# Softmax factors of three head pairs: from a fan copy and four transposes to one transpose, a store to DRAM and two reads

## The chip, the cores and the metric

The kernel runs on one core of one Trainium2 chip. The metric is the device time of one execution in microseconds (us). The core's engines are TensorE (PE; its weight loads are PEld), VectorE (DVE), ScalarE (ACT), GpSimd (POOL) and SyncE (SP). SyncE, GpSimd and ScalarE also issue DMAs; SyncE's and ScalarE's go through hardware queues (q1 and q10 in the profile), GpSimd's through the software queue (q0). All of them are served by the same 16 DMA engines.

## The reference

One layer of a hybrid encoder over 512 positions of width 1024, in float32:

```
h = rms_norm(x, attn_norm_g)
xr, gate, q, k, v = split(h @ w_in)
y_rnn  = (rg_lru forward + rg_lru backward of conv(xr)) * gelu(gate)
y_attn = dilated_attention(q, k, v, rel_bias)        # 8 heads of 64, three windows each
x = x + concat(rms_norm(y_rnn), rms_norm(y_attn)) @ w_out
x = x + square(relu(rms_norm(x) @ w_up)) @ w_down
return rms_norm(x, final_norm_g)
...
# inside dilated_attention, for each window (offs, bias):
logits = q . k[gathered] * scale + bias;  lse = logsumexp(logits)
out_w = softmax(logits) . v[gathered]
# the windows are joined with the weights softmax(lse)
o = sum_w softmax(lse)_w * out_w
```

Joined with those weights, the three windows are one softmax over all gathered keys. The kernel computes it so: exponentials of all keys, their product with v, and at the end one division by the row's sum. The factor of that division, one number for each position and head, is what this case is about.

## The kernel before, in words

Matrix products are made in three passes of split operands (`whi`, `wlo` and the like, lines 329 to 331). ScalarE makes the high part of each weight tile (L274), VectorE the low part (L282), and SyncE streams the raw tiles in (L241), a fixed number ahead. The order of instructions on PE, ACT, DVE and POOL is the order in which the code is written (`manual_schedule`); SyncE's order is set by a scheduler, and is fixed in the built program.

The attention part handles heads in pairs, p = 0 to 3. A loop over i (0 to 4) and u (0 to 3) interleaves three stages: the scores and exponentials of pair i (`att_s`, `att_f`, `att_e`), the transposes of pair i-1 (`att_t`) and the product of pair i-1 with the values (`att_av`, at the end of step u = 3). Between them `fill` puts single steps of other matrix products (`pqk`, `pwr`) on TensorE. `pt`, `prow` and, for pairs 0 and 1, `pav` share two PSUM banks; `pav` and `prow` of the later pairs share two others.

The factors of a pair p take this way. The exponentials leave their sums in `zs[p]`, 128 rows (positions) by 8 columns (4 blocks of positions by 2 heads).

- `att_z(p)`, at step (p+1, 0): VectorE takes the reciprocal `rz` (128x8) and fans each column out 64 times into `rzb` (128x512, L854).
- `att_r(p)`, at step (p+1, 1): TensorE transposes `rzb` in four blocks of 128x128 into the bank `prow` (L408), and ScalarE copies it to `zrow[p]` (128x512, L861). Row r of `zrow` now holds, along its 512 positions, the factor of the head that row r of the value product belongs to.
- `att_av(p)`, at step (p+1, 3): 32 matmuls make the value product `pav`; then VectorE multiplies it with `zrow[p]` into `yp` (L952, in `av_y`). For pair 2 this multiplication is put off to step (4, 0), behind the next pair's first transposes (`late_y`). ScalarE squares and scales `yp` (L598, L957).

For pair 3 VectorE's order is: product of pair 2 (L952), reciprocal of pair 3 (L852), fan copy of pair 3 (L854); TensorE's transposes of pair 3 (L408) wait for that copy.

Other transfers in the same stretch: `load_x` (L1081 to L1089) loads residual tiles and builds three sums of weight blocks in the tile `ws`, with loads on SyncE and accumulating DMAs on GpSimd; `sum_s4` (L1094, L1095) copies one of them inside `ws` on SyncE and accumulates on GpSimd; `load_tw` (L479, L480) loads the bias rows `tb`; `load_t` (L1198, L1200) loads weights of the next stage.

Of the kernel before, what the change touches and what calls it, by code (L numbers as in the profile page):

```python
# [12 lines left out]
FT = mybir.dt.float32  # L13
FR = mybir.dt.float32r
AF = mybir.ActivationFunctionType
OP = mybir.AluOpType

P = 128
S = 512
# [3 lines left out]
DH = 64  # L23
# [86 lines left out]
def hybrid_kernel(ctx: ExitStack, tc, xw, xn, w_in, w_v, w_out, w_up, w_dn, gates, vecs, rel, onehot, fg, out):  # L110
    nc = tc.nc
# [4 lines left out]
    dram = ctx.enter_context(tc.tile_pool(name="dram", bufs=1, space=bass.MemoryType.DRAM))  # L116
# [3 lines left out]
    act = nc.scalar.activation  # L120
# [3 lines left out]
    def g_(name, dt=FT, shape=(P, S)):  # L124
        return work.tile(list(shape), dt, name=name, tag="g", bufs=NG)

    def small(name, w):
        return work.tile([P, w], FT, name=name, tag="sm%d" % w, bufs=8)

    def ps_(name, tag):  # L130
        return psum.tile([P, S], FT, name=name, tag=tag, bufs={"pj": 4, "gs": 2, "et": 2}[tag])
# [15 lines left out]
    ident = consts.tile([P, P], FT, name="ident")  # L147
# [253 lines left out]
    def fan(t, c, n, w):  # L401
        base = t[:, c:c + 1]
        return bass.AP(tensor=base.tensor, offset=base.offset, ap=[base.ap[0]] + ([[1, n]] if n > 1 else []) + [[0, w]])

    def rows_of(cols, tag):
        pr = ps_("prow", tag)
        for tt in range(4):
            nc.tensor.transpose(pr[:, tt * P:(tt + 1) * P], cols(tt), ident)  # L408
        return pr
# [74 lines left out]
    halves = (slice(0, 64), slice(64, 128))  # L484
# [284 lines left out]
    et, en, zs = {}, {}, {}  # L769
# [78 lines left out]
    zrow, rzbs = {}, {}  # L848

    def att_z(p):  # L850
        rz = small("rz", 8)
        nc.vector.reciprocal(rz, zs.pop(p))  # L852
        rzb = g_("rzb")
        nc.vector.tensor_copy(rzb, fan(rz, 0, 8, DH))  # L854
        rzbs[p] = rzb

    def att_r(p):
        rzb = rzbs.pop(p)
        pr = rows_of(lambda tt: rzb[:, tt * P:(tt + 1) * P], "et" if p < 3 else "gs")
        zrow[p] = g_("zrow")  # L860
        act(zrow[p], pr, AF.Copy)  # L861

    def att_y(p):
# [289 lines left out]
    for i in range(5):  # L1153
        for u in range(4):
# [20 lines left out]
            if u == 0 and i >= 1:  # L1175
                att_z(i - 1)
# [4 lines left out]
            if u == 1 and i >= 1:  # L1181
                att_r(i - 1)
# [85 lines left out]
    for w in OSEQ:  # L1268
        for i in range(4):
            tt, k = i // 2, i % 2  # L1270
# [253 lines left out]
    for half in range(2):  # L1524
# [169 lines left out]
        for j in range(7 * NQ):  # L1694
            _, w, q = seq[j]
# [31 lines left out]
        if half == 1:  # L1727
# [27 lines left out]
            pr = ps_("pd", "pj")  # L1755
# [60 lines left out]
```

## Time and profile before

| | before |
|---|---|
| median of 3 runs (lowest, highest) | 531.61 us (530.47, 531.9) |
| the profiled execution's own time | 532.29 us |
| its span, first to last instruction | 530.5 us |
| mean granted TensorE clock | 0.997 |
| DMA in the span | 35740 packets, 108.30 MB, mean 204 GB/s |
| queues, share of 16 engines' span | q1 41.1%, q0 32.1%, q10 1.3% |

The attention part lies between about 100 and 185 us of the span. In a row of a timeline the columns are start (us), duration (us), engine, line and operation, output<-input, count, and in brackets the idle time before it with what ended it; a row ending in a larger count merges instructions, and its duration runs from the first to the last. The `q` behind an engine's name (SPq) means its DMA queue: the row is the issue of a DMA, not its transfer. A row of waits reads: who waited, for whom, us in total, times, longest. A row of windows gives for a stretch the busy us of PE, PEld, DVE, ACT and POOL with their counts, then the granted clock, the share of the DMA engines and GB/s. A row of the chain gives start, duration and what was running. In the chain a matmul's time ends with its result, so its rows stand up to 0.2 us behind those of the timeline.

### The profile page before, as it was taken

Reading aid. Unit: us, or ns where it says so; the run is one execution under the profiler, and the core shown is the slowest. Engines: PE = TensorE matmul, PEld = TensorE weight load, DVE = VectorE, ACT = ScalarE, POOL = GpSimd, SP = SyncE. Lnnn points to the kernel's source line nnn. Section 1 sums busy time; section 2 is a strip of 40 time slices with the busy share of each in tenths; the row PEclk is TensorE's granted clock in tenths of the full one; section 3 lists DMA queues with packets and bytes.
Section 4 is the critical chain, followed back from the end, with each engine's and each line's share of the span. In section 5 each row is a group of like instructions: output and inputs, shape, how many; then the busy total and the mean of one; then the engine's idle time right before and its main releaser. Section 6 shows DMA issues by size and latency. Waiting matters only on the chain.

```text
span 530.5 us, 9181 instructions
## 1 busy us (share of the span) xinstructions
PE 521.1 (98%) x3495; PEld 446.4 (84%) x3495; DVE 431.0 (81%) x710; ACT 361.1 (68%) x569; POOL 66.8 (13%) x96
## 2 busy tenths in 40 slices
PE   8999999999999999999999999999999999999995
PEld 7855888877777878899999888888999999888884
DVE  5799589588779898898779986879756987987885
ACT  7566968578678867586477755575567677655654
POOL 3340000000202121001210222001101200131000
PEclk9999999999999999999999999999999999999998
DMA  8798165585567989948395999986968496799704
GB/s 309 256 236 217 41 152 159 164 150 179 105 220 153 331 196 256 371 146 229 100 214 144 228 272 274 311 289 140 291 209 228 107 223 207 163 299 263 174 1 159
DMA packets 35740, 108.30 MB, mean 204 GB/s; under 512 B 4109, under 2 KB 7082, under 8 KB 35696
## 3 DMA queue, kind: packets, MB, share of 16 engines
q1 hardware_dynamic: 26000, 74.66, 41.1%
q0 software_dynamic: 8784, 31.76, 32.1%
q10 hardware_dynamic: 912, 1.30, 1.3%
q8 instruction: 27, 0.44, 0.3%
q14 instruction: 17, 0.14, 0.1%
HBM read 98.24 MB, written 4.21 MB: 193 GB/s over the span
## 4 chain that ended last, share of the span: by engine, by line
PE 92%; ACT 2%; DMA 2%; DVE 2%; SPq 1%; issue 0%; DVEq 0%; ACTq 0%
PE pu L331 10%; PE pu L330 10%; PE pu L329 10%; PE pd L330 10%; PE pd L331 10%; PE pd L329 9%; PE pqk L329 3%; PE pqk L331 3%; PE pqk L330 3%; PE pt L841 2%; PE pav L928 2%; PE pv L329 1%; PE pn L787 1%; PE pp L331 1%; PE pp L329 1%; PE pp L330 1%
## 5 line engine op out<-in xcount | busy, mean ns | idle before, releaser
L282 DVE TENSOR_TENSOR wlo<-wraw,whi 128x1024 fp32r<-128x1024 f32 x72 | 87.8, 1221 | 26.4 <-ACT whi L274 26.2
L274 ACT ACTIVATE whi<-wraw 128x1024 fp32r<-128x1024 f32 x69 | 72.9, 1058 | 41.1 <-PE pd L331 20.5
L330 PE MATMUL pd<-wlo,ah 128*128 128x512 f32 (+1 forms) x195 | 75.4, 386 | 0.0
L329 PE MATMUL pd<-whi,ah 128*128 128x512 f32 (+1 forms) x195 | 75.3, 386 | 0.0
L331 PE MATMUL pd<-whi,al 128*128 128x512 f32 (+1 forms) x195 | 75.3, 386 | 0.0
L274 ACT ACTIVATE whi<-tw 128x1024 fp32r<-128x1024 f32 x40 | 42.3, 1059 | 38.0 <-DMA tw<-in_w_up_dram 11.1
L331 PE MATMUL pu<-hh,wlo 128*128 128x256 f32 x224 | 63.5, 284 | 0.0
L330 PE MATMUL pu<-hl,whi 128*128 128x256 f32 x224 | 63.5, 284 | 0.0
L329 PE MATMUL pu<-hh,whi 128*128 128x256 f32 x224 | 63.5, 283 | 0.0
L282 DVE TENSOR_TENSOR wlo<-tw,whi 128x1024 fp32r<-128x1024 f32 x40 | 48.9, 1223 | 17.9 <-ACT whi L274 17.9
L329 PE MATMUL pu<-h2h,whi 128*128 128x256 f32 (+1 forms) x200 | 60.2, 301 | 0.0
L331 PE MATMUL pu<-h2h,wlo 128*128 128x256 f32 (+1 forms) x200 | 60.1, 301 | 0.0
L330 PE MATMUL pu<-h2l,whi 128*128 128x256 f32 (+1 forms) x200 | 60.1, 301 | 0.0
L329 PEld LDWEIGHTS pu<-hh,whi 128*128 128x128 f32 x224 | 43.1, 192 | 0.0
L330 PEld LDWEIGHTS pu<-hl,whi 128*128 128x128 f32 x224 | 43.1, 192 | 0.0
L331 PEld LDWEIGHTS pu<-hh,wlo 128*128 128x128 f32 x224 | 43.1, 192 | 0.0
L329 PEld LDWEIGHTS pd<-whi,ah 128*128 128x128 f32 x195 | 36.7, 188 | 7.4
L330 PEld LDWEIGHTS pd<-wlo,ah 128*128 128x128 f32 x195 | 36.6, 188 | 7.3
L331 PEld LDWEIGHTS pd<-whi,al 128*128 128x128 f32 x195 | 36.7, 188 | 7.3
L274 ACT ACTIVATE whi<-ts 128x1024 fp32r<-128x1024 f32 x24 | 25.5, 1061 | 24.7 <-PE pd L331 18.5
L330 PEld LDWEIGHTS pu<-h2l,whi 128*128 128x128 f32 x200 | 38.3, 192 | 1.3
L331 PEld LDWEIGHTS pu<-h2h,wlo 128*128 128x128 f32 x200 | 38.3, 192 | 1.3
(286 smaller groups left out, 1232.8 us busy)
## 6 DMA issues: line engine op xcount, KB each, us to landing
wraw<-in_w_up_dram SPq DMA_DIRECT2D x25, 512.0 KB
ts<-in_w_dn_dram POOLq DMA_DIRECT2D x24, 512.0 KB, 13.5
wraw<-in_w_dn_dram SPq DMA_DIRECT2D x24, 512.0 KB
tw<-in_w_up_dram SPq DMA_DIRECT2D x15, 512.0 KB
tw<-in_w_up_dram POOLq DMA_DIRECT2D x15, 512.0 KB, 8.3
wraw<-in_w_in_dram SPq DMA_DIRECT2D x13, 512.0 KB
ts<-in_w_dn_dram SPq DMA_DIRECT2D x8, 512.0 KB
tw<-in_w_dn_dram SPq DMA_DIRECT2D x8, 512.0 KB
```

The source lines that it names most:

```text
L274: act(hi, raws[i], AF.Copy)
L282: nc.vector.tensor_tensor(lo, r, f(splits[i][0]), op=OP.subtract)
L329: nc.tensor.matmul(o, lhsT=a[0], rhs=b[0], start=bool(first), stop=False, skip_group_check=on)
L330: nc.tensor.matmul(o, lhsT=a[0], rhs=b[1], start=False, stop=False, skip_group_check=on)
L331: nc.tensor.matmul(o, lhsT=a[1], rhs=b[0], start=False, stop=bool(last), skip_group_check=on)
L787: nc.tensor.matmul(pnear[p][e][r, o:o + k1 - k0], lhsT=q, rhs=raw[p, 1][halves[e], k0:k1], start=u == u0, stop=True, skip_group_check=True)
L841: nc.tensor.transpose(pt[:, i * P:(i + 1) * P], en[h][u][:, c * P:(c + 1) * P], ident)
L928: nc.tensor.matmul(o(half[e]), lhsT=v[:, h * DH:(h + 1) * DH], rhs=c(et[h, x]), start=first, stop=last, skip_group_check=True)
```

## The change

For pairs 0, 1 and 2 the fan copy goes. `rz` (128x8) is transposed once into 8 rows of 128; ScalarE copies these 8x128 numbers to `zt`; a DMA stores them in a small DRAM tile `zd` (4 KB); and two DMAs, one for each head, read them back into `zrow[p]`, each with 64 rows that all read the same 4 blocks of 128 numbers (the first step of the source is 0). The DMAs are issued by GpSimd for pairs 0 and 1 and by SyncE for pair 2. Pair 3 stays as it was.

```diff
     def att_z(p):
         rz = small("rz", 8)
         nc.vector.reciprocal(rz, zs.pop(p))
+        if p < 3:
+            rzbs[p] = rz
+            return
         rzb = g_("rzb")
         nc.vector.tensor_copy(rzb, fan(rz, 0, 8, DH))
         rzbs[p] = rzb
 
+    zd = [dram.tile([8, P], FT, name="zd%d" % i) for i in range(3)]
+
     def att_r(p):
         rzb = rzbs.pop(p)
-        pr = rows_of(lambda tt: rzb[:, tt * P:(tt + 1) * P], "et" if p < 3 else "gs")
         zrow[p] = g_("zrow")
+        if p < 3:
+            pr = ps_("prow", "et")
+            nc.tensor.transpose(pr[:8, :P], rzb, ident)
+            zt = g_("zt", shape=(8, S))
+            act(zt[:, :P], pr[:8, :P], AF.Copy)
+            q = nc.gpsimd if p < 2 else nc.sync
+            q.dma_start(zd[p], zt[:, :P])
+            for e in range(2):
+                q.dma_start(zrow[p][halves[e]].rearrange("p (u q) -> p u q", u=4),
+                            bass.AP(tensor=zd[p].tensor, offset=zd[p].offset + e * P, ap=[[0, DH], [2 * P, 4], [1, P]]))
+            return
+        pr = rows_of(lambda tt: rzb[:, tt * P:(tt + 1) * P], "gs")
         act(zrow[p], pr, AF.Copy)
```

On SyncE's queue, before, the copy inside `ws` is followed at once by loads of weights (`wraw`, `tw`):

```order
L1094 DMA ws_1769<-ws_1769 128x1024
L241 DMA wraw_1981<-in_w_out_dram 128x1024
L1198 DMA tw_2351<-in_w_up_dram 128x1024
L241 DMA wraw_2051<-in_w_out_dram 128x1024
L1198 DMA tw_2376<-in_w_up_dram 128x1024
```

And now, with the store and the two reads of pair 2 (L871, L873; lines behind the edit are 16 higher):

```order
L1110 DMA ws_1770<-ws_1770 128x1024
L871 DMA zd2_873<-zt_1970 8x128
L873 DMA zrow_1967<-zd2_873 64x4x128 x2
L241 DMA wraw_1981<-in_w_out_dram 128x1024
L1214 DMA tw_2351<-in_w_up_dram 128x1024
L241 DMA wraw_2051<-in_w_out_dram 128x1024
```

The three DMAs of pair 2 stand behind the copy inside `ws` and ahead of the weight loads; the reads wait for the store's landing, and the weight loads stand behind both.

On GpSimd's queue, before, from the sums for the recurrent half (`tw`) to the sums in `ws`:

```order
L1050 DMA tw<-in_w_out_dram 128x1024 x3
L289 DMA tw<-in_w_out_dram 128x1024
L1050 DMA tw<-in_w_out_dram 128x1024
L416 TENSOR_TENSOR rcol_1610<-rv,mhalf 128x4
L1089 DMA ws<-in_w_out_dram 128x1024 x4
```

And now:

```order
L1066 DMA tw<-in_w_out_dram 128x1024 x3
L871 DMA zd_871<-zt 8x128
L873 DMA zrow<-zd_871 64x4x128 x2
L289 DMA tw<-in_w_out_dram 128x1024
L1066 DMA tw<-in_w_out_dram 128x1024
L416 TENSOR_TENSOR rcol_1610<-rv,mhalf 128x4
L871 DMA zd_872<-zt 8x128
L873 DMA zrow<-zd_872 64x4x128 x2
L1105 DMA ws<-in_w_out_dram 128x1024 x4
```

Pair 0's three DMAs stand ahead of the accumulate of L289, pair 1's ahead of the four accumulates into `ws`.

On VectorE, around the product of pair 2 (`yp_2099`; `rz_2101` and `rzb_2103` are of pair 3, which keeps its fan copy), as it stands now:

```order
L1054 SCALAR_TENSOR_TENSOR x1_1765<-pwr_2054,nrc0_1612,x1_1765 128x512
L968 TENSOR_TENSOR yp_2099<-pav_2068,zrow_1967 128x4x4x32
L852 RECIPROCAL rz_2101<-zz_1885 128x8
L857 COPY rzb_2103<-rz_2101 128x512
L282 TENSOR_TENSOR wlo_2130<-wraw_1368,whi_2062 128x1024
```

This row of instructions is the same as before; only the operand `zrow` of the product now comes from a DMA.

## The prediction

> **What bounds the kernel now.** I read the page's busy times first, then its chain, then the waits of SyncE's DMA queue, then the timeline around the four products that use the softmax factors.
>
> ```profile
> PE 521.1 (98%) x3495; PEld 446.4 (84%) x3495; DVE 431.0 (81%) x710; ACT 361.1 (68%) x569; POOL 66.8 (13%) x96
> ...
> PE 92%; ACT 2%; DMA 2%; DVE 2%; SPq 1%; issue 0%; DVEq 0%; ACTq 0%
> ```
>
> TensorE is busy for 98% of the span and is 92% of the chain that ended last. So only two things move the end: instructions taken off TensorE, and new waits of TensorE. Work taken off VectorE or ScalarE pays only where TensorE waits for it. The span is 530.5 us, the profiled execution's own time 532.29 us, the median of the three runs 531.61 us. I make the sum against 532.29 and take 0.68 off at the end.
>
> **What the change takes off TensorE.** The chain, in order of time, prices the transposes:
>
> ```profile
> 173.43 0.87 PE pt L841 x8
> ...
> 174.99 0.44 PE prow L408 x4
> ```
>
> Four transposes add 0.44 us to TensorE's stream, eight add 0.87 us, so one is 0.11 us. Each of the pairs 0, 1 and 2 loses three of four: 0.33 us a pair, about 1.0 us in all. The remaining one streams the same 128 columns of the identity and is priced the same.
>
> **What it takes off VectorE and ScalarE.** These rows, of a timeline of all engines, hold the fan copy (L854) and what surrounds the product of pair 2:
>
> ```profile
> 172.03 1.10 DVE L952 TENSOR_TENSOR yp<-pav,zrow 128x512 f32<-128x512 f32 x1
> ...
> 172.96 0.18 DVE L852 RECIPROCAL rz<-zz 128x8 f32<-128x8 f32 x1
> 173.19 0.43 DVE L854 COPY rzb<-rz 128x512 f32<-128x512 f32 x1
> ...
> 174.39 0.86 POOL L1095 DMA_DIRECT2D ws<-in_w_out_dram  x1 [9.64 <-DMA ws<-ws]
> ...
> 174.83 0.60 PE L408 MATMUL prow<-ident,rzb 128*128 128x128 f32 x4
> ```
>
> Three copies of 0.43 us go, and three ScalarE copies of 128x512 (about 0.6 us each) become copies of 8x128. TensorE is not waiting for either there, so I price both at nothing. Their cover is TensorE's own row of matmuls.
>
> **What it adds.** The factors reached the product's operand zrow by one ScalarE copy. Now they take three DMAs in sequence: a store of 4 KB, and two reads of 128 KB (256 pieces of 512 B each), which can be issued only after the store has landed. When the copy ran, and when pairs 0 and 1 needed it:
>
> ```profile
> 123.44 0.65 ACT L861 ACTIVATE zrow<-prow 128x512 f32<-128x512 f32 x1
> ...
> 143.74 0.65 ACT L861 ACTIVATE zrow<-prow 128x512 f32<-128x512 f32 x1
> ...
> 163.50 0.57 ACT L861 ACTIVATE zrow<-prow 128x512 f32<-128x512 f32 x1
> ```
>
> ```profile
> 133.65 1.11 DVE L952 TENSOR_TENSOR yp<-pav,zrow 128x512 f32<-128x512 f32 x1 [0.67 <-PE pav L928]
> ...
> 154.46 1.10 DVE L952 TENSOR_TENSOR yp<-pav,zrow 128x512 f32<-128x512 f32 x1 [0.67 <-PE pav L928]
> ```
>
> **Pairs 0 and 1, on GpSimd's queue.** From the start of the small copy to the product there are 10.2 us for pair 0 and 10.7 us for pair 1; the value products come 0.3 us earlier by the transposes saved, so 9.9 and 10.4 us. The nearest rows for a small transfer issued by GpSimd:
>
> ```profile
> oht<-in_onehot_dram POOLq DMA_DIRECT2D x1, 145.5 KB, 3.7
> oht<-in_onehot_dram POOLq DMA_DIRECT2D x1, 97.0 KB, 3.5
> ```
>
> The copy ends 0.3 us after it starts, the store takes 3.5, the second read is issued some 0.6 us after the first and takes 3.7: about 8.1 us. That leaves 1.8 us for pair 0 and 2.3 us for pair 1, so I price them at 0. What lies behind them on GpSimd's queue has room: the accumulate at L289 was issued at 132.85 and those at L1089 from 152.72. Bounds: nothing below. Above, a read of 9.0 us (a row below) ends pair 0 about 3.5 us late; VectorE then holds the bank of pav from the next transposes, and TensorE stands.
>
> **Pair 2, on SyncE's queue.** The order above shows its store behind the copy ws<-ws, which SyncE held back by 15.6 us until an accumulate had landed:
>
> ```profile
> SPq L1094 <- DMA ws<-in_w_out_dram: 15.6, 1, 15.6
> ```
>
> ```profile
> 167.62 0.53 SPq L1094 DMA_DIRECT2D ws<-ws  x1
> 168.25 0.72 SPq L241 DMA_DIRECT2D wraw<-in_w_out_dram  x1
> ```
>
> So although the factors of pair 2 are ready at about 163.8, their store starts at 167.6 at the earliest (167.62 + 0.53, less 0.6 for the transposes saved by then). The product ran at 172.03 without a wait in front of it. Four microseconds must hold a store and two reads.
>
> How long the store takes, no row says. The quick end is a store of 12 KB on an idle queue, whose reader waited for it:
>
> ```profile
> 64.30 0.91 ACTq L471 DMA_DIRECT2D nbd<-nbs  x2
> ```
>
> ```profile
> 65.76 1.30 SPq L479 DMA_DIRECT2D tb<-nbd  x2
> ```
>
> That is 1.5 us. The slow end is the transfer that this store directly follows in the same queue: ws<-ws was issued at 167.62, and GpSimd, which waited for its landing alone, went on at 174.39, so 6.8 us. The DMA engines are full there:
>
> ```profile
> 168.00:170.00 2.00, 2.00 (x22) 1.50 (x23) 2.00 (x7) 2.00 (x6) 0.00 (x0) 1.00 1.03 203
> ```
>
> With a share of 1.03 and a transfer of 512 KB ahead, I take the slow end: the store lands with ws<-ws, at 167.0 + 6.8 = 173.8. [...]
>
> For the reads the quick end is the 3.5 us above. The slow end is a bias read on SyncE's queue (tb, 128 KB in pieces of 1 KB) in another full stretch:
>
> ```profile
> 109.63 0.52 SPq L479 DMA_DIRECT2D tb<-nbd  x1
> ...
> 114.09 10.46 SPq L241 DMA_DIRECT2D wraw<-in_w_out_dram  x2
> ```
>
> ```profile
> SPq L241 <- DVE wlo L282: 5.5, 1, 5.5
> SPq L241 <- DMA tb<-nbd: 4.2, 1, 4.2
> ```
>
> The second of the two wraw issues waited 4.2 us for that tb from about 114.4, to 118.6: 9.0 us after its issue. I take 3.5, since everything else on SyncE's queue is now held back behind the reads. The second read is issued 0.5 us after the first, so zrow is whole at 173.8 + 0.5 + 3.5 = 177.8.
>
> Then the product, the reciprocal and the fan copy of pair 3 follow on VectorE, 1.6 us from 172.03 to 173.62, and the transposes of pair 3 (174.83 on TensorE) wait for that copy. They start at 179.4 + 0.06, which is **4.6 us later** than before. The 1.0 us saved on TensorE is inside this difference. Queued behind the product on VectorE are a weight split (wlo) and a residual update, whose readers come after those transposes; queued on ScalarE are the square and scaling of that product. On SyncE the weight loads that started from 168.25 start from about 175; the first is converted at 178.57, which moves to 183, and the rest later. I add nothing for them.
>
> Sum: 532.29 + 4.6 = 536.9, less 0.68 gives **536.2 us**. With the ends (169.1 or 173.8 for the store, 3.5 or 9.0 for the read), the shift lies between -0.1 and +10.1 us.
>
> **The rivals.**
>
> *The round trip is quick enough.* If the store passes ws<-ws and lands 1.5 us after its issue, the reads are whole at 173.1, pair 3's copy ends at 174.7, and TensorE, which is there at 173.85, stands 0.9 us, nearly what it has saved: 531.5. It decides at a landing of zrow near 173.2. For it: only 4 KB. Against it: 6.8 us for the transfer ahead and a full DMA share. [...]
>
> *No wait at all.* Only the transposes count: 531.61 - 1.0 = 530.6, within what a measurement here can tell from no change (0.3%, 1.6 us).
>
> *The clock falls in the stall.* TensorE would stand for about 5 us. At the end of the kernel the granted clock fell some 3.2 us after the last matmul (at 524.03; 0.63 over a microsecond is a fall at 527.26):
>
> ```profile
> 524.00:525.00 1.00, 0.03 (x1) 0.00 (x0) 0.96 (x5) 0.32 (x2) 0.00 (x0) 1.00 0.39 148
> ...
> 527.00:528.00 1.00, 0.00 (x0) 0.00 (x0) 0.00 (x0) 0.00 (x0) 0.00 (x0) 0.63 0.98 357
> 528.00:529.00 1.00, 0.00 (x0) 0.00 (x0) 0.00 (x0) 0.00 (x0) 0.00 (x0) 0.50 0.54 167
> ```
>
> If matmuls then run at half clock for as long as it took to fall, 3.2 us, half of that is lost: 1.6 us more, 537.8. No row shows how long the clock takes to recover, or whether a stall inside the kernel starts it. [...]
>
> *Pair 0 is late too.* Its reads run at 127 to 132, beside four residual loads and four bias reads of SyncE. If the second takes 6.5 us, pair 0 is about 1 us late and all of it lands on TensorE: 537.2.
>
> **How the numbers follow.** Stall at pair 2 alone: 0.50 (533.5 to 540). With the clock falling: 0.17, about a quarter of the stall's cases, since the one fall in the trace came after 3.2 us and the stall is little longer. With pair 0 late as well: 0.10. Quick round trip: 0.17. No wait: 0.06. The two last lie inside 530.0 to 533.2 but for a small tail, and the first three above it: faster 0.04, same 0.19, slower 0.77. The range takes in the quick round trip partly and the stall to 9 us: 531.2 to 540.8.
>
> **What the profile after would show.** Right: the product of pair 2 waits for a DMA of zrow for 4 to 7 us; the transposes of pair 3 wait for the fan copy; the store of pair 2 is issued within a microsecond after ws<-ws, and the reads 5 us or more later; products 0 and 1 wait for TensorE as before. Wrong: the reads of pair 2 issued by 170, or no wait before that product, or a wait at products 0 or 1 that is larger than that at product 2.

## The result and the profile after

| | before | after |
|---|---|---|
| median (lowest, highest) | 531.43 us (530.47, 531.9; 6 runs) | 544.62 us (541.87, 548.01; 6 runs) |
| ratio, with its 95% interval | | 1.0251 (1.0226 to 1.0275) |
| profiled execution's own time, span | 532.29 us, 530.5 us | 541.87 us, 540.1 us |
| mean granted clock of that execution | 0.997 | 0.991 |

The change costs 13.2 us in the medians, where the prediction had 4.6. The profiled execution of after is its lowest, that of before (532.29 us) lies above all six timed runs of its kernel, so the two profiles differ by 9.6 us only.

The busy times of the page after, and the shares of its chain:

```profile
PE 521.5 (97%) x3486; PEld 446.7 (83%) x3486; DVE 429.8 (80%) x707; ACT 360.9 (67%) x569; POOL 72.3 (13%) x102
...
PE 91%; DMA 4%; ACT 1%; DVE 1%; issue 0%; SPq 0%; DVEq 0%; ACTq 0%
```

TensorE is as busy as before in microseconds although nine transposes are gone (3495 and 3486 records), because some of its matmuls now run at half clock: the granted clock is 0.50 from 179.1 to 185.9 us, and the four transposes of pair 3 take about 418 ns each there, where before they take 272. DMA has doubled its share of the chain. The waits of VectorE and TensorE that are new:

```profile
DVE yp L968 <- DMA zrow<-zd: 13.6, 2, 10.1
...
PE prow L408 <- DVE rzb L857: 8.8, 1, 8.8
PE pt L841 <- DVE yp L968: 1.7, 1, 1.7
```

VectorE waits twice for the reads. TensorE's 1.7 us stand behind the product of pair 0 (the bank of `pav` comes free late), its 8.8 us behind that of pair 2 (pair 3's fan copy follows that product). The chain shows both places, in order of time:

```profile
128.08 6.13 DMA zrow<-zd
134.29 1.09 DVE yp L968
135.43 0.66 PE pt L841 x4
...
167.44 5.89 DMA zd<-zt
173.48 0.66 SPq L873
174.19 6.62 DMA zrow<-zd
180.93 1.08 DVE yp L968
182.08 0.44 DVE rzb L857
182.56 1.11 PE prow L408 x4
```

At pair 2 the store lands 5.9 us after its issue, the second read 6.6 us after its own. At pair 0 the reads are issued 5.3 us after the store, by these rows of GpSimd's timeline:

```profile
122.12 0.56 POOL L871 DMA_DIRECT2D zd<-zt  x1 [81.62 <-DMA tb<-nbd]
127.41 1.30 POOL L873 DMA_DIRECT2D zrow<-zd  x2 [4.73 <-DVE rsum L1001]
```

The second row names VectorE's `rsum` as what ended the wait. By the times it was the store: in the change the issue follows the store's last packet (126.3) by 1.1 us, and in eight kernels with this order, the change's included, it lies anywhere from 0.2 us before the end of `rsum` to 0.6 us behind it.

Four transposes behind a wait take 0.66 us at pair 0 and 1.11 us at pair 3. The windows say why (the column behind the five engines is the granted clock, then the DMA share and GB/s):

```profile
173.00:174.00 1.00, 0.79 (x4) 0.32 (x3) 0.00 (x0) 0.79 (x2) 0.33 (x1) 1.00 0.00 0
...
178.00:179.00 1.00, 0.00 (x0) 0.00 (x0) 0.00 (x0) 0.00 (x0) 0.00 (x0) 1.00 1.03 205
179.00:180.00 1.00, 0.00 (x0) 0.00 (x0) 0.00 (x0) 0.00 (x0) 0.00 (x0) 0.54 1.14 270
...
185.00:186.00 1.00, 1.00 (x5) 0.86 (x4) 0.52 (x2) 0.68 (x3) 0.00 (x0) 0.55 1.03 422
186.00:187.00 1.00, 1.00 (x7) 0.56 (x5) 0.59 (x2) 1.00 (x4) 0.00 (x0) 1.00 1.05 414
```

TensorE's last matmul ends at about 173.8. The clock falls to 0.50 at about 179.1, 5.3 us later, and comes back at about 185.9, 3.3 us after the matmuls resume at 182.56.

Two theories stood after this reading. A: the loss is two waits, a long one on SyncE's queue at pair 2 and a short one at pair 0, plus the clock that falls in the long one. B: a trip through DRAM costs wherever it is taken. In A it was open whether pair 2's lateness comes from its place in the queue or from reads that are slow in themselves, and what makes them slow.

### The profile page after: what moved, and what is told of

It reads as the page before. It is cut to its first block, busy times and chain, and to the rows that moved or that the text cites. A ratio compares the mean times of both kernels' runs of the same rounds, so it can differ in the third digit from the quotient of the medians.

```text
span 540.1 us, 9186 instructions
## 1 busy us (share of the span) xinstructions
PE 521.5 (97%) x3486; PEld 446.7 (83%) x3486; DVE 429.8 (80%) x707; ACT 360.9 (67%) x569; POOL 72.3 (13%) x102
## 4 chain that ended last, share of the span: by engine, by line
PE 91%; DMA 4%; ACT 1%; DVE 1%; issue 0%; SPq 0%; DVEq 0%; ACTq 0%
PE pu L329 10%; PE pu L331 10%; PE pu L330 10%; PE pd L329 9%; PE pd L330 9%; PE pd L331 9%; PE pqk L329 2%; PE pqk L331 2%; DMA zrow<-zd 2%; PE pqk L330 2%; PE pt L841 2%; PE pg L519 2%; PE pv L329 2%; PE pv L330 1%; PE pv L331 1%; PE pp L331 1%
## 5 line engine op out<-in xcount | busy, mean ns | idle before, releaser
L329 PEld LDWEIGHTS pu<-h2h,whi 128*128 128x128 f32 x200 | 38.3, 191 | 1.3
```

The lines of the kernel that those rows point to most:

```text
L329: nc.tensor.matmul(o, lhsT=a[0], rhs=b[0], start=bool(first), stop=False, skip_group_check=on)
```

## The experiments

Every ratio below is against the kernel before, timed beside it on the same chip.

### Which pair carries the loss

One part alone, three times. The condition in `att_z` and `att_r` is changed:

```diff
-        if p < 3:
+        if p < 2:      # pairs 0 and 1; in the two others  p == 2  and  p == 1
```

> Pairs 0 and 1 take the way through DRAM on GpSimd's queue, pair 2 keeps its fan copy and four transposes. Theory A (SyncE's queue at pair 2 carries nearly all of the loss, pair 0 carries one short stall of 1.7 us): six transposes less, -0.7 us, and the product of pair 0 about 1.7 us late, so about 532.4 us, between 531.3 and 533.5; no wait of VectorE or TensorE longer than 1 us between 165 and 190 us of the span. Theory B (the added traffic of the reads, or the way through DRAM as such, costs the same for every pair): a third to two thirds of the loss of 13 us is here, 536 to 540 us.

> Only pair 2 takes the way through DRAM, on SyncE's queue; pairs 0 and 1 are as before. Theory A: three transposes less (-0.3 us), TensorE stands about 8.8 us ahead of pair 3's transposes, the clock falls in that stall and costs about 1.7 us: +10 us, 541.5 us, between 539 and 545. Theory B (each pair carries its share): 536 us or less.

> Only pair 1 takes the way through DRAM, on GpSimd's queue, in a stretch where the DMA engines have little to do. All theories that put the loss on pairs 0 and 2: three transposes less, nothing waits, 0.3 us below the kernel before, which the runs cannot tell from no change. If the way through DRAM costs wherever it is taken: 533 us or more.

| | median | ratio |
|---|---|---|
| pairs 0 and 1 | 534.01 us | 1.0054 (1.0034 to 1.0074) |
| pair 2 | 544.35 us | 1.0251 (1.0230 to 1.0271) |
| pair 1 | 531.20 us | 0.9991 (0.9981 to 1.0001) |

Pair 2 alone has the whole ratio of the change, and pair 1 alone costs nothing. Pairs 0 and 1 lose 3.1 us, half a microsecond above the upper end that theory A gave. The two losses (13.4 and 3.1 us) do not add up to the change's 13.2. Part of that shows in the profiles: TensorE stands 9.3 us ahead of pair 3's transposes with pair 2 alone, 8.8 us in the change, where pair 0 has made it late already. The rest is not shown. The waits of that profile, which is its lowest run (532.64 us):

```profile
DVE yp L968 <- DMA zrow<-zd: 3.8, 1, 3.8
...
PE pt L841 <- DVE yp L968: 1.9, 1, 1.9
```

One wait for `zrow`, at pair 0, and 1.9 us of TensorE behind it. Theory B falls with pair 1: the same DMAs on the same queue, in a stretch where the DMA engines have little to do (in the change a share of 0.29 from 144 to 150 us, against 0.80 from 122 to 127 and 0.70 from 127 to 134 at pair 0), and no loss.

### The place on SyncE's queue

The copy `ws<-ws`, behind which pair 2's store stands, is issued by GpSimd instead:

```diff
-        nc.sync.dma_start(s4, s2)
+        nc.gpsimd.dma_start(s4, s2)
```

> The changed kernel with the copy inside ws issued by GpSimd, so that pair 2's store and reads stand on SyncE's queue behind nothing that waits. Theory A (the place in the queue, behind ws<-ws, is the cause): the store is issued at about 163 us, zrow is whole by 172 to 174, the product of pair 2 waits 0 to 2 us, the clock does not fall; with pair 0's 1.7 us and the 1.0 us saved the time is 532 to 534 us. Theory C (store and reads are slow in this stretch wherever they stand, 6 us each): zrow whole at about 176, TensorE stands 3 us or more, 535 to 538 us.

Measured: 536.40 us, ratio 1.0097 (1.0080 to 1.0114). In the timeline:

```profile
163.59 0.31 SPq L871 DMA_DIRECT2D zd<-zt  x1
165.58 1.36 SPq L873 DMA_DIRECT2D zrow<-zd  x2
...
177.14 1.08 DVE L968 TENSOR_TENSOR yp<-pav,zrow 128x512 f32<-128x512 f32 x1 [5.22 <-DMA zrow<-zd]
```

With nothing ahead of it the store lands within 2.0 us. But the reads, issued 8 us sooner than in the change, are whole only at 177.1, 10.2 us after the second was issued (165.58 + 1.36), and VectorE still waits 5.2 us for them. The place in the queue is half of the story. Theory C has the other half, the slow reads, but not the store, which it put at 6 us. What the DMA engines did from 166 to 174 us (queue, kind, packets, MB, share of 16 engines; q0 is GpSimd's, q1 SyncE's):

```profile
q0 software_dynamic: 387, 1.44, 94.0%
q1 hardware_dynamic: 245, 0.12, 7.9%
```

GpSimd's transfers, the accumulates into `ws` and from 169 the copy, take 94% of the engines' time, in packets of 3.7 KB on average that hold an engine 0.31 us each (0.94 x 16 x 8 / 387). SyncE's packets of 0.5 KB need 0.04 us each, and 245 of the reads' 512 pieces get through in 8 us.

### What makes the reads slow

Two runs. The first takes the competitor away: the changed kernel without the two DMAs of GpSimd that start with pair 2's reads.

```diff
-        nc.gpsimd.dma_start(s4, oblock("21"), accum_op=OP.add)
...
-        nc.gpsimd.dma_start(lo, raws[i], accum_op=OP.add)   # for the weight block s2 only
```

> The changed kernel without two of GpSimd's DMAs, the accumulate of a weight block into ws behind ws<-ws and the accumulating copy tw<-ws (512 KB each), so the weights built from them lack a term. In the changed kernel these run from 175 us, beside the reads of pair 2. Theory F (the reads are slow because the DMA engines are held by those accumulates): the reads land about 3.5 us after the last issue, as pair 1's did in a quiet stretch (3.2), not 6.6; TensorE stands about 6 us instead of 8.8, and the time is 2.5 to 4.5 us lower, 540 to 542 us. Theory E (a read of one small DRAM tile by 64 rows is slow of itself on SyncE's queue, or slowed by SyncE's own weight loads behind it): 6 us or more for the reads, and the time as with the change, 543.5 us or more.

Measured: 539.98 us, ratio 1.0152 (1.0133 to 1.0170), against 1.0251 for the change.

```profile
175.53 1.32 SPq L875 DMA_DIRECT2D zrow<-zd  x2
...
179.65 1.08 DVE L970 TENSOR_TENSOR yp<-pav,zrow 128x512 f32<-128x512 f32 x1 [6.76 <-DMA zrow<-zd]
```

The second read is issued by 176.85 and the product runs at 179.65, 2.8 us later instead of 6.1 by the same rows of the change (174.79 and 180.93). TensorE stands 5.5 us there instead of 8.8. Theory F holds: the accumulates made the reads slow. SyncE's own weight loads are issued behind the reads here too, and the reads took 2.8 us all the same.

The second makes the reads into fewer pieces. The reciprocal is written with the two heads apart, so that the 4 KB in DRAM lie by head and each of the 64 rows reads one piece of 2 KB:

```diff
-        nc.vector.reciprocal(rz, zs.pop(p))
+        nc.vector.reciprocal(rz.rearrange("p (e t) -> p t e", e=2), zs.pop(p).rearrange("p (t e) -> p t e", e=2))
...
-            bass.AP(tensor=zd[p].tensor, offset=zd[p].offset + e * P, ap=[[0, DH], [2 * P, 4], [1, P]]))
+            bass.AP(tensor=zd[p].tensor, offset=zd[p].offset + e * 4 * P, ap=[[0, DH], [1, 4 * P]]))
```

> The changed kernel with the factors stored in another order, so that each of the 64 rows of a read takes one piece of 2 KB instead of four of 512 B: the same bytes in a quarter of the pieces. Theory D (on each DMA engine the pieces of SyncE's queue take turns with the pieces of GpSimd's accumulates, which take 0.31 us each, so a read is as slow as it has pieces): the reads of pair 2 land 2 to 3 us sooner than the 6.6 us after the last issue, pair 0's 1.7 us go too, the store's 5.9 us stay; TensorE still stands 5 to 7 us; 539 to 542 us. Theory E (the reads are slow by their bytes, or by their place): the same as the changed kernel, 544 to 546 us.

> Both: pieces of 2 KB, and the copy inside ws on GpSimd's queue, so that the store stands behind nothing. Theory D: store 2 us, reads about 4.5 us instead of 10.2, zrow whole at about 171.5, before the product of pair 2 comes up; pair 0 waits 0 to 1 us; the 1.0 us of the nine transposes is what is left: 530 to 531.5 us, level with the kernel before or a little faster. Theory E: as with the copy on GpSimd's queue alone, 536.4 us.

Measured: 541.51 us, ratio 1.0187 (1.0166 to 1.0209), with the larger pieces alone; 534.16 us, ratio 1.0042 (1.0026 to 1.0058), with `ws<-ws` on GpSimd as well. Both intervals lie below those of the same kernel with small pieces (1.0251 and 1.0097): about 3 us each. Both profiled executions were the slowest of their kernel, and they don't show where the gain is. With the larger pieces alone the product runs 6.1 us after the last issue has ended and TensorE stands 8.9 us, as in the change; theory D had expected 5 to 7. In the second run the forecast was too good by 3 us, because the product still waited: the store, with nothing ahead of it in its queue, took 4.3 us (163.98 to 168.32) instead of 2, and the reads 6.8 us instead of 4.5.

The packets say what the reads waited for. In the second run the reads are issued from 168.32 on, and until 172.2 not one packet of SyncE's queue passes. The queues from 168.4 to 172.2 us:

```profile
q0 software_dynamic: 211, 0.80, 106.0%
```

The change has the same gap between its two reads. By 176.6 as many packets have passed as the first read has pieces, 256; the second read, issued by 174.8, has none until 178.9, while GpSimd's accumulate and accumulating copy fill the engines. From 176.7 to 178.6 us:

```profile
q0 software_dynamic: 90, 0.37, 98.2%
```

The copy `ws<-ws` itself, issued at 166.81 in the change, has no packet before 170.7, while GpSimd's accumulates fill the engines (213 packets, 104.8%), and the store's packets pass from 172.57 on, among the last of `ws<-ws`. Once SyncE's packets pass, they pass beside GpSimd's: with `ws<-ws` on GpSimd it is 245 beside 333 from 167 to 174 us. Whether each engine takes turns packet by packet, as theory D assumed, these counts do not show. Why these three transfers of SyncE's, issued beside GpSimd's accumulates, began only about 4 us after their issue (168.32 to 172.2, 174.8 to 178.9, 166.81 to 170.7), where the reads of the run without the two accumulates, with GpSimd moving nothing, began 1.4 us after theirs (175.53 to 176.9), no run here shows. Nor does a trace show what the larger pieces gain.

### What the fall of the clock costs

Extra matmuls ahead of pair 3's transposes, 24 in one run and 48 in another:

```diff
-        pr = rows_of(lambda tt: rzb[:, tt * P:(tt + 1) * P], "gs")
+        pr = ps_("prow", "gs")
+        for _ in range(24):
+            nc.tensor.matmul(pr[:, :P], lhsT=ones, rhs=ones, start=True, stop=True)
+        for tt in range(4):
+            nc.tensor.transpose(pr[:, tt * P:(tt + 1) * P], rzb[:, tt * P:(tt + 1) * P], ident)
```

> The changed kernel with 24 extra matmuls of 128x128 (their result is overwritten) on TensorE directly ahead of pair 3's transposes, where it stands idle. They make the idle stretch of TensorE shorter and the wait for the factors no shorter. Theory A (the clock falls about 5 us after the last matmul, and the half clock afterwards costs 1.7 us): the granted clock stays at 1.00 from 175 to 190 us and the time is about 1.7 us below that of the changed kernel, 543 us where that has 544.6. Theory B (the clock is not what costs, the 11 us are all waiting): the same time as the changed kernel or, by the extra matmuls, more.

> The changed kernel with 48 extra matmuls instead of 24 ahead of pair 3's transposes: 24 lasted only 5.0 us of an 11 us stretch, 48 last about 10. Theory A (the fall of the clock costs 1.7 to 3 us): the granted clock stays at 1.00 from 175 to 192 us, pair 3's transposes start as late as without them or up to 1 us later, and the time is 1 to 2.5 us below the changed kernel: 541.5 to 543.5 us. Theory B (half the clock for a few us costs nothing that counts): 544.6 us or more.

With 24 they ended at 181.6, the clock fell at 183.9 all the same, and half clock lasted 5.5 us after the matmuls resumed: 547.11 us, ratio 1.0298 (1.0276 to 1.0320), slower than the change. That run failed as a test of the clock. Its profile is slow at pair 0 too: from pair 0's product to pair 1's it takes 20.9 us (135.29 to 156.16), the change 19.4 (134.29 to 153.72), and VectorE waits there 2.0 us for TensorE's `pqk`, in the change 0.6. Whether that is why it is 2.5 us slower is not shown. With 48 the clock stayed at 1.00: 543.22 us, ratio 1.0232 (1.0215 to 1.0248). The medians alone do not tell that from the change. The traces do. From pair 3's transposes to pair 3's product is the same work in every kernel; first with 48 extra matmuls, then with the change:

```profile
185.37 0.66 PE L880 MATMUL prow<-ident,rzb 128*128 128x128 f32 x4 [0.47 <-DVE rzb L857]
...
191.41 1.10 DVE L972 TENSOR_TENSOR yp<-pav,zrow 128x512 f32<-128x512 f32 x1
```

```profile
182.56 1.11 PE L408 MATMUL prow<-ident,rzb 128*128 128x128 f32 x4 [8.77 <-DVE rzb L857]
...
189.85 1.12 DVE L968 TENSOR_TENSOR yp<-pav,zrow 128x512 f32<-128x512 f32 x1 [0.22 <-PE pav L944]
```

6.0 us at full clock, 7.3 us in the change; the kernel before has 6.2 (174.83 to 181.06). So the half clock costs 1.1 to 1.3 us in the profiled execution. In the run with pair 2 alone, where the half clock lasts to 189.0, the same stretch takes 8.4 us (183.09 to 191.53).

### Does starting earlier help?

The reciprocal is ready about 3 us before its transpose. The transpose is moved up, for all three pairs:

```diff
-            if u == 1 and i >= 1:
+            if u == (1 if i == 4 else 0) and i >= 1:
                 att_r(i - 1)
```

> The changed kernel with the transpose and the small copy of pairs 0, 1 and 2 moved from step (p+1, 1) to the end of step (p+1, 0), some 3 us earlier, where the reciprocal has just been made. Pair 0 gets 3 us more of room, and its 1.7 us stall should go. Pair 2's store stays behind ws<-ws on SyncE's queue, so theory A (its place in the queue sets when it starts) expects nothing there: the store is still issued after ws<-ws, at about 167.5, and TensorE still stands 8 to 9 us: about 543 us, 541.5 to 544. If pair 2's loss hangs on when its factors are ready, its stall shrinks by 3 us too: 540 us or less.

> Early transposes, and the copy inside ws on GpSimd's queue; reads in pieces of 512 B as in the change. Pair 2's store can go at about 159.5, before the three accumulates into ws fill the DMA engines (from 163), and lands by 161.5; the reads are issued by 163 and land by 166 to 172 even at the slowest speed seen (10.2 us); the product comes up at 172. No wait for zrow at any of the three pairs, no fall of the clock. What is left is the gain of nine transposes, about 1 us: 530 to 530.8 us where the kernel before has 531.2. If the reads collide with the accumulates and run over 10 us, 531.5 to 534.

> As the run with early transposes and the copy on GpSimd's queue, and with pieces of 2 KB too. If that run has no wait left, this one is the same, 530 to 530.8 us; if it still waits for reads in some executions, this one is 0.5 to 2 us faster and its executions lie closer together.

| | median | ratio |
|---|---|---|
| early | 548.97 us | 1.0319 (1.0294 to 1.0343) |
| early, `ws<-ws` on GpSimd | 537.58 us | 1.0106 (1.0084 to 1.0128) |
| early, `ws<-ws` on GpSimd, 2-KB pieces | 536.26 us | 1.0082 (1.0068 to 1.0096) |

All three missed. In the first, pair 2 behaved as theory A said: its store still stood behind `ws<-ws`, and TensorE stood 8.6 us there. In the last two no product waits for `zrow` at all, and yet they lose 4 to 6 us. The waits and GpSimd's timeline of the second kernel show a new place:

```profile
DVE nrc L616 <- POOL rcol L416: 7.6, 1, 7.6
...
PE pn L787 <- DVE mn L826: 4.0, 1, 4.0
```

```profile
137.87 0.56 POOL L871 DMA_DIRECT2D zd<-zt  x1 [4.55 <-ACT zt L869]
142.87 1.28 POOL L873 DMA_DIRECT2D zrow<-zd  x2 [4.45 <-DMA zd<-zt]
144.17 1.06 POOL L416 TENSOR_TENSOR rcol<-rv,mhalf 128x4 f32<-128x4 f32 x1
```

In the change the same operation of GpSimd stands ahead of pair 1's store, which is issued at 143.94:

```profile
138.55 1.05 POOL L416 TENSOR_TENSOR rcol<-rv,mhalf 128x4 f32<-128x4 f32 x1 [6.09 <-DVE rv L413]
```

GpSimd ran these in the order of the code. The earlier transpose put pair 1's store and reads ahead of `rcol`, which the recurrent half needs. GpSimd stood 4.45 us for the store's landing, `rcol` ran at 144.17 instead of 138.55, VectorE waited 7.6 us for it, and TensorE 4.0 us for VectorE. The clock fell too, to 0.50 from about 147.4 to 150.8, when the matmuls had already resumed (146.56).

What stayed open was whether waits account for the whole loss. So pair 1 was put back, and only pairs 0 and 2 left early:

```diff
-            if u == 1 and i >= 1:
+            if u == (0 if i in (1, 3) else 1) and i >= 1:
```

> Early transposes for pairs 0 and 2 only, and the copy inside ws on GpSimd's queue; pair 1 stands behind rcol on GpSimd again. If the waits at pairs 0 and 2 (and the clock in them) are the whole loss, no wait for zrow, for rcol or of pair 3's transposes is left, and the nine transposes show: 0.6 to 1.2 us below the kernel before, 530.0 to 531 us where that has 531.5. If the way through DRAM or the moved copy costs something else as well, 532.5 us or more with no such wait in the trace.

> The same with pieces of 2 KB. With no wait left it should be level with the run without them, 530.0 to 531 us; a gain of over 0.5 us would say that reads still end late in some executions.

> Pairs 0 and 1 through DRAM with pair 0's transpose early; pair 2 and the copy inside ws as in the kernel before. Six transposes less, 0.7 us, and pair 0's wait, which cost 3 us in the run with pairs 0 and 1, gone: 530.5 to 531 us where the kernel before has 531.5. If 533 us or more again, that loss was not the wait for zrow.

| | median | ratio |
|---|---|---|
| pairs 0 and 2 early, `ws<-ws` on GpSimd | 530.33 us | 0.9974 (0.9963 to 0.9984) |
| the same, 2-KB pieces | 530.48 us | 0.9975 (0.9964 to 0.9986) |
| pairs 0 and 1 only, pair 0 early | 530.66 us | 0.9981 (0.9970 to 0.9991) |

All three times came out as expected. They are only 0.2 to 0.3% below the kernel before, but the interval of each ends below 1. The products of pairs 0, 1 and 2 in the first:

```profile
133.22 1.09 DVE L968 TENSOR_TENSOR yp<-pav,zrow 128x512 f32<-128x512 f32 x1 [1.99 <-DMA zrow<-zd]
152.65 1.11 DVE L968 TENSOR_TENSOR yp<-pav,zrow 128x512 f32<-128x512 f32 x1 [0.69 <-PE pav L944]
169.72 1.10 DVE L968 TENSOR_TENSOR yp<-pav,zrow 128x512 f32<-128x512 f32 x1
```

Pair 0 still waits 2.0 us on VectorE, but no longer holds up TensorE, whose list has no wait behind `yp` or `rzb`; its busy share is 99%, where the kernel before has 98%. The trip at pair 0 is no shorter than in the change, 15 us from the store's issue (117.98) to the product against 12; it starts 4 us earlier. With no wait on TensorE left the change is worth 1.4 us (0.9 to 2.0 by the interval). The way through DRAM costs nothing else that these runs can tell.

## Why the prediction was wrong

The direction, the place and the chain of waits at pair 2 were right; three terms of the sum were too small, and the reason given for the largest of them was wrong.

- **Nine transposes, -1.0 us: right.** The repaired kernel gains 1.4 us (0.9 to 2.0 by its interval), the one with six transposes less 1.0 us.
- **Pairs 0 and 1 at 0: right for pair 1, wrong for pair 0.** The store was taken at 3.5 us and the reads at 3.7, from transfers of GpSimd at another time. At pair 0, beside the residual loads and bias reads, the reads are issued 5.3 us after the store (122.12 to 127.41) and land 6.1 us later. TensorE stands 1.7 us in the profile; in the runs with pairs 0 and 1 alone the loss is 3.1 us in the median, and it goes when pair 0 starts earlier. What slows pair 0's trip no run isolates. At pair 1, in a quiet stretch, the reads can be issued 2.2 us after the store (143.94 to 146.14), and nothing waits. The rival "pair 0 is late too" was right.
- **Pair 2's store: right.** Issued at 167.44 behind `ws<-ws`, landed at 173.33, against 173.8. Without that transfer ahead it took 2.0 us in one run and 4.3 us in another, beside GpSimd's accumulates.
- **Pair 2's reads at 3.5 us: the step that failed.** They took 6.6. The reason given was that everything else on SyncE's queue is held back behind them. That was true, and the windows show the DMA engines idle from 173 to 175 (shares of 0.00 and 0.03). But it looked at one queue only. The landing of `ws<-ws`, right ahead of the store's, also releases GpSimd's accumulate into `ws` and its accumulating copy `tw<-ws`; the first of them stands in the prediction's own timeline (174.39). They start beside the reads, and the second read has no packet until 178.9. Without them the product runs 3.4 us after the second read's issue (176.2), where the prediction took 3.5.
- **The clock: put down as a rival at 0.17, and it happened.** Its price, 1.6 us, is close to the 1.1 to 1.3 us measured. The chance was too low: the clock fell in or just behind all eleven profiled stalls of TensorE of 3.0 to 9.3 us in this study, that of 3.0 us in the run with `ws<-ws` on GpSimd and larger pieces included, not in a quarter of them. It fell at a shorter one as well, of 1.8 us at pair 0 in the run without the two accumulates, where the matmuls of `pqk` behind it take 0.63 us instead of 0.39 to 0.40. At that of 2.2 us in the run with 24 extra matmuls VectorE's wait for `pqk` says the same (2.0 us, against 1.7 in the run without the two accumulates); behind six others of 1.3 to 1.9 us that wait is 0.55 to 0.56 us.

The sum of after's profile is then 1.7 + 8.8 + 1.1 - 1.0 = 10.6 us. That execution was 1.9 us ahead before the change is reached (SyncE issued the bias read that stands at 109.63 in the profile of before at 107.69), which leaves 8.7 of the 9.6 us between the profiles. The other 0.9 us, and why the other five executions are 1.7 to 6.1 us slower than the profiled one, are not shown by any trace; their granted clocks, 0.983 to 0.991, say that they have at least as much half clock.

## What to carry to other kernels

What this round trip through DRAM cost was set by what shared the DMA engines in its own 10 us, not by its bytes: look for every transfer that is released by the same event as yours, on every queue, and give the trip the room of its slow case. Before a step that waits for a landing is put on an engine that works its list in order, as GpSimd did here (`rcol` at 144.17 instead of 138.55), or moved up on it, read what then stands behind it there. Once no wait was left, the one microsecond of TensorE that the change aimed at was really there.

## What the runs showed of the hardware that I had not expected

- Two reads of 128 KB in 512-B pieces took 2.8 us after the last issue had ended where GpSimd moved nothing, 6.1 us beside its accumulate and accumulating copy, and 10.2 us behind and beside its three accumulates into `ws`. A 4 KB store with nothing ahead of it in its queue took 2.0 us when it was issued 0.4 us behind the first of the same accumulates, and 4.3 us when it was issued 1.1 us behind it. Behind a copy of 512 KB it took 5.9 us.
- The granted clock fell to 0.50 5.3 us after TensorE's last matmul in the change, 3.4 us in the run with `ws<-ws` on GpSimd (174.8 to 178.2), and 2.1 us in the run with larger pieces (174.7 to 176.8). It returned 2.8 to 5.9 us after the matmuls resumed. Ten falls inside the kernels stand whole in the windows: four lasted 3.4 us (`ws<-ws` on GpSimd with small and with larger pieces, the run without the two accumulates, early with `ws<-ws` on GpSimd), three 6.8 us (the change, 24 extra matmuls, the first of early) and three 10.2 us (pair 2 alone, larger pieces alone, the second of early). In two of them the matmuls had resumed before the clock fell (178.19 and 179.0 with `ws<-ws` on GpSimd and larger pieces, 146.56 and 147.4 in early with `ws<-ws` on GpSimd). What sets these times no run shows.
